# Expert stages of a two-layer block in 12 and 9 units instead of 15 and 10, with products, scatter and gather each in whole runs and six static experts in layer 1

## The chip, the cores and the metric

One core of a Trainium2 chip runs the whole program. The metric is the device time of one execution in microseconds, as the median of three runs. Names of engines: PE is the matrix engine, DVE the vector engine, ACT the scalar engine, POOL the general engine; SP only issues transfers here.

## The reference

Two layers over 256 context rows and 256 latent rows of width 1024. Each layer is a mixer (an RWKV scan in layer 0, differential attention in layer 1) followed by a mixture of experts, and the change is in the experts alone:

```
pg = softmax(h @ router_g + router_g_b)             # 4 groups, the best one is kept
el = (h @ router_e + router_e_b) of that group      # 8 experts, the best two are kept
for g, e:                                           # 32 experts of 1024 -> 256 -> 1024
    hid = silu(h @ w_gate[g, e]) * (h @ w_up[g, e])
    y  += (hid * gates[:, g, e]) @ w_down[g, e]
```

Layer 0 puts 512 rows through this, layer 1 only the 256 latent rows. So 1024 and 512 pairs of row and expert are spread unevenly over 32 experts. An expert's weights are 3 MB in float32, those of a layer 96 MB, and all of them are read in every execution.

## The kernel before

**Units.** An expert gets a fixed number of places (slots) in a unit of 128 places. A unit of kind S holds one expert with 128 slots, P two with 64, Q four with 32. `ORDER` (line 275) gives the kinds in the order of work: 15 units in layer 0, 10 in layer 1. Experts are taken by their rank: the first `STATIC` ones (2 in layer 0, 4 in layer 1) are the experts 0, 1, ... themselves, known when the program is built; the others follow by falling count of rows, and which expert that is only the router tells. What does not fit its slots goes through a loop (`beyond`, from line 2164) with one pass per 64 rows, serial, after the stage.

**Work of a unit.** `onehots` (DVE) compares ranks with slot numbers. `gather` (PE, tile `gp`, line 1862) copies the unit's rows out of the hidden state by products with these one-hot matrices, two units at a time, high and low part of each value apart (`HI`, `LO`), and ACT copies the result into `XG`. `up` (PE, tile `pg`, line 1885) makes the gate and up products in eight steps k of 128 rows each; experts of one unit lie in different column groups of the array, so the four products of a Q step run side by side. `act` (ACT silu, DVE product) gives `hs`, `turn` (PE, tile `ht`) transposes it, `down` (PE, tile `po`, line 1913) makes the last product in two halves, and ACT and DVE scale it into a high and a low part `OB`. `places` (DVE) builds the one-hot matrix `OT` and the gates from `SB` and `WB`, which the rest of the router delivers (`so`, then four PE transposes into `bp`, line 2031). `scatter` (PE, tile `yp`, line 1948, two matmuls per k) brings the unit's output back to the rows, and DVE adds it to `H` (line 1956), for the last units to the block's output `X` (`join`, line 1941).

**Order of the work.** The order is written out by hand in the loop at the end of `moe` and each engine keeps it. In step k of unit s the PE does `up` of s, then `scatter` step k of unit s-2, then one gather step of a coming unit; `turn` and `down` of unit s-1 are put in at k = 1 to 4. The last two units are scattered together.

**Weights.** A load is a third of an expert, 1 MB: c = 0 and 1 are the gate and up weights of four steps each, c = 2 the down weights. All loads go through SP's queue in one order (`expert_loads`) into a ring of buffers, and a load waits until the last reader of the buffer before it is done. In layer 0 the ring has 8 buffers (line 1633). For layer 1 line 1592 adds buffers of the attention stage, 14 in all:

```
more = [(wp, "ah", 2), (wp, "whi", 4)]
ring.pools = more[:1] * 2 + [more[1], ring.pools[0]] * 4 + ring.pools[4:]
```

Loads of static experts are issued before the stage, up to the ring's size; those of the others first read the expert's number (`ids`, DVE cast at line 1801) into a register of SP.

Of the kernel before, what the change touches and what calls it, by code (L numbers as in the profile page):

```python
# [130 lines left out]
STATIC = (2, 4)  # L131
# [143 lines left out]
ORDER = ("PPQSSQSPQSPPPPP", "PPPQQQQQQP")  # L275
# [4 lines left out]
def expert_units(layer):  # L280

    if layer == 1:
        one = []
        two = [(2 * i, 2, 64, 128 * i) for i in range(4)]
        four = [(8 + 4 * i, 4, 32, 512 + 128 * i) for i in range(6)]
    else:
        one = [(2 + i, 1, 128, 128 + 128 * i) for i in range(4)]
        two = [(0, 2, 64, 0)] + [(6 + 2 * i, 2, 64, 640 + 128 * i) for i in range(7)]  # L290
        four = [(20 + 4 * i, 4, 32, 1536 + 128 * i) for i in range(3)]
    kinds = dict(S=one, P=two, Q=four)
    return [kinds[c].pop(0) for c in ORDER[layer]]


def expert_loads(layer):

    us = expert_units(layer)
    out = [(us[0][0], j, 0) for j in range(us[0][1])]
    for n, u in enumerate(us):  # L300
        last = us[n + 1:][:1]
        for v, c in [(u, 1)] * (n + 1 < len(us)) + [(v, c) for v in last for c in range(2 if n + 2 == len(us) else 1)]:
            out += [(v[0], j, c) for j in range(v[1])]
        out += [(u[0], j, 2) for j in range(u[1])]
    return out
# [21 lines left out]
class Prog:  # L327
# [1289 lines left out]
    def open_ring(self):  # L1617
# [21 lines left out]
        def experts(layer, n=32):  # L1639
            return [(load, (layer, r0 + j, c), A["wexp"][layer, r0 + j, :, c * 2048:(c + 1) * 2048])  # L1640
                    for r0, j, c in expert_loads(layer) if r0 < n]
# [13 lines left out]
    def moe(self, layer, TT):  # L1655
# [10 lines left out]
        with ExitStack() as es:  # L1666
# [19 lines left out]
            def rows(i, hf):  # L1686
                tag = ("gu", "gu", "xg", "ht", "po", "po", "y", "gu")[hf * NT + i]
                if tag != "po":
                    tp = pp.tile([P, 512], F32, name="htp", tag=tag, bufs=2 if tag in ("gu", "y") else 1)
# [24 lines left out]
            rp = pp.tile([P, 5, 32], F32, name="rp", tag="y", bufs=2)  # L1714
# [61 lines left out]
            def by_count():  # L1776
# [14 lines left out]
                rt = pp.tile([32, TT], F32, name="rt", tag="y", bufs=2)  # L1791
# [5 lines left out]
                pr = pp.tile([P, NT, 32], F32, name="pr", tag="y", bufs=2)  # L1797
                ip = pp.tile([1, 32], F32, name="ip", tag="y", bufs=2)
# [3 lines left out]
                for i in range(NT):  # L1802
# [4 lines left out]
                ring.todo[i:i + 1] = [(load_dyn, r0 + j, c) for r0, j, c in expert_loads(layer)  # L1807
                                      if r0 >= STATIC[layer]]
# [4 lines left out]
                base = st("base", 32)  # L1813
                if layer == 0:
                    s2, s6, s20 = (st(f"s{n}", 32) for n in (2, 6, 20))
                    for t, n, f in ((s2, 2.0, -64.0), (s6, 6.0, 64.0), (s20, 20.0, 32.0)):
                        nc.vector.tensor_scalar(t, pos, n, f, op0=OP.is_ge, op1=OP.mult)
                    nc.vector.scalar_tensor_tensor(shift, s2, 64.0, s6, op0=OP.add, op1=OP.add)
                    nc.vector.tensor_tensor(shift, shift, s20, OP.add)
                    nc.vector.tensor_scalar(base, shift, -1.0, 128.0, op0=OP.mult, op1=OP.add)  # L1820
                    nc.vector.tensor_tensor(base, base, pos, OP.mult)
                    nc.vector.scalar_tensor_tensor(base, s2, -64.0, base, op0=OP.add, op1=OP.add)
                    nc.vector.scalar_tensor_tensor(base, s6, 5.0, base, op0=OP.mult, op1=OP.add)
                    nc.vector.scalar_tensor_tensor(base, s20, 19.0, base, op0=OP.mult, op1=OP.add)
                else:
                    s8 = own
                    nc.vector.tensor_scalar(s8, pos, 8.0, 32.0, op0=OP.is_ge, op1=OP.mult)
                    nc.vector.tensor_scalar(shift, s8, 64.0, None, op0=OP.add)
                    nc.vector.tensor_scalar(base, shift, -1.0, 128.0, op0=OP.mult, op1=OP.add)
                    nc.vector.tensor_tensor(base, base, pos, OP.mult)  # L1830
                    nc.vector.tensor_scalar(base, base, 64.0, None, op0=OP.subtract)
                    nc.vector.scalar_tensor_tensor(base, s8, 7.0, base, op0=OP.mult, op1=OP.add)
# [6 lines left out]
            def onehots(n):  # L1839
# [4 lines left out]
                r0, nj, w, _ = shapes[n]  # L1844
                of = rkp if r0 >= STATIC[layer] else rk
                o = OHs[g][:, :, h * P:(h + 1) * P].rearrange("p n (e c) -> p n e c", c=w)
                for i in range(NT):
                    nc.vector.tensor_tensor(o[:, i], self.cst("iota")[:, None, 0:w].to_broadcast([P, nj, w]),
                                            of[:, i, r0:r0 + nj, None].to_broadcast([P, nj, w]), OP.is_equal)
# [352 lines left out]
```

## Time and profile before

| | |
|---|---|
| median of 3 runs | 1619.13 us (1616.69 to 1620.01) |
| the profiled execution, its span | 1621.09 us, 1619.3 us |
| PE busy | 1462.1 us (90%) |
| DVE, ACT, POOL busy | 888.7, 602.0, 225.3 us |
| granted PE clock, mean | 0.963 |
| moved by DMA | 355.80 MB, 220 GB/s on average |
| experts of layer 0 | from 779.6 us (first `pg`) to 1109.7 us (last `X`) |
| experts of layer 1 | from 1370.3 us to 1613.4 us, output stored after that |

The span is that of the instructions on the core; the execution's own time is 1.8 us more. Everything between the two expert stages (attention) and before the first is the same in both kernels.

### The profile page before, as it was taken

What the parts mean: (1) busy time and instruction counts of PE and PEld (TensorE: products, weight loads), DVE (VectorE), ACT (ScalarE), POOL (GpSimd) and SP (SyncE); (2) the same over time, 40 slices, a digit from 0 to 9 for tenths busy, and PEclk for the clock granted to TensorE, in tenths of its full rate; (3) what the DMA queues carried; (4) which work ended last, traced back from release to release, by engine and by line L of the source; (5) the groups of instructions that cost most, each with busy time, mean ns of one, the idle gap of its engine ahead of it and who ended that gap; (6) DMA issues with size and microseconds to landing.
All of it is one profiled execution on the core that took longest, in us unless ns stands there. A gap on an engine that the chain in (4) does not pass through costs nothing. (4 is left out here: it accounts for less than half of the span.)

```text
span 1619.3 us, 28356 instructions
## 1 busy us (share of the span) xinstructions
PE 1462.1 (90%) x10935; PEld 785.8 (49%) x10935; DVE 888.7 (55%) x2200; ACT 602.0 (37%) x1260; POOL 225.3 (14%) x345
## 2 busy tenths in 40 slices
PE   5778989999999999988999999986999998998787
PEld 1224445455554565444645445422888885432223
DVE  1746773778778877324735545575555544342224
ACT  3333516355564654324211111105677763211011
POOL 0631212132332331202000000000200001000000
PEclk8999998999999989999999999998999997999999
DMA  8256785766646622343488878782020253799996
GB/s 359 112 199 214 223 268 162 230 203 193 207 158 216 197 85 86 99 135 157 157 329 320 363 293 359 289 330 88 27 102 25 84 183 141 299 373 420 421 421 262
DMA packets 102602, 355.80 MB, mean 220 GB/s; under 512 B 12096, under 2 KB 36032, under 8 KB 74560
## 3 DMA queue, kind: packets, MB, share of 16 engines
q1 hardware_dynamic: 100944, 352.37, 58.9%
q8 instruction: 88, 1.44, 0.4%
q10 hardware_dynamic: 1520, 1.58, 0.3%
q14 instruction: 50, 0.41, 0.1%
HBM read 342.90 MB, written 11.01 MB: 219 GB/s over the span
## 5 line engine op out<-in xcount | busy, mean ns | idle before, releaser
L1885 PE MATMUL pg<-ring,XG 128*32 128x512 f32 (+2 forms) x1024 | 236.1, 615 | 18.5 <-DMA ring<-in_wexp 17.0
L639 PE MATMUL prj<-mxs,wj 128*128 128x512 f32 x288 | 163.4, 650 | 7.0 <-DMA mxs<-mixed 6.9
L1956 DVE TENSOR_TENSOR H<-H,yp 128x512 f32<-128x512 f32 (+1 forms) x152 | 88.7, 588 | 133.8 <-PE yp L1948 133.4
L1948 PE MATMUL yp<-OT,OB 128*128 128x512 f32 (+1 forms) x400 | 129.4, 414 | 2.6 <-DVE X L1941 1.4
L1913 PE MATMUL po<-ring,HT 128*32 128x512 f32 (+2 forms) x512 | 110.2, 622 | 16.2 <-DMA ring<-in_wexp 11.5
L1948 PEld LDWEIGHTS yp<-OT,OB 128*128 128x128 f32 x400 | 61.9, 188 | 118.9 <-issue 45.4
L1917 DVE SCALAR_TENSOR_TENSOR OB<-po,gate,OB 128x512 fp32r<-128x512 f32 x50 | 37.5, 751 | 118.8 <-ACT OB L1916 118.8
L1916 ACT ACTIVATE OB<-po,gate 128x512 fp32r<-128x512 f32 x50 | 34.4, 688 | 180.0 <-PE po L1913 180.0
L1862 PE MATMUL gp<-OH,HI 128*128 128x256 f32 (+1 forms) x352 | 97.5, 308 | 0.0
L996 ACT COPY UV<-pc 64x64 f32<-64x64 f32 x256 | 53.0, 207 | 109.2 <-PE pc L585 86.7
L1862 PE MATMUL gp<-OH,LO 128*128 128x256 f32 (+1 forms) x352 | 89.5, 286 | 0.0
L1862 PEld LDWEIGHTS gp<-OH,HI 128*128 128x128 f32 x352 | 68.7, 195 | 41.3 <-issue 36.2
L1014 POOL TENSOR_SCALAR es<-S,E 128x64 f32<-128x64 f32 x96 | 52.1, 552 | 247.8 <-DVE S L1009 189.8
L367 PE MATMUL gv_ps<-wmod,cst_c 128*32 128x256 f32 (+1 forms) x704 | 62.6, 431 | 25.5 <-DMA wmod<-in_wmod 24.9
L1885 PEld LDWEIGHTS pg<-ring,XG 128*32 128x32 f32 (+2 forms) x1024 | 45.7, 124 | 77.1 <-DMA ring<-in_wexp 36.0
L1866 ACT COPY XG<-gp 128x512 f32<-128x512 f32 (+1 forms) x56 | 30.3, 540 | 124.8 <-PE gp L1862 124.8
L1862 PEld LDWEIGHTS gp<-OH,LO 128*128 128x128 f32 x352 | 69.0, 196 | 2.9 <-issue 1.9
L932 DVE TENSOR_TENSOR xt<-L,X 128x126 f32<-128x126 f32 (+22 forms) x248 | 66.8, 270 | 6.2
L934 DVE TENSOR_TENSOR X<-X,xt 128x126 f32<-128x126 f32 (+22 forms) x248 | 65.1, 263 | 9.0
L639 PEld LDWEIGHTS prj<-mxs,wj 128*128 128x128 f32 x288 | 44.9, 192 | 42.7 <-issue 28.7
L1913 PEld LDWEIGHTS po<-ring,HT 128*32 128x32 f32 (+2 forms) x512 | 28.2, 126 | 71.6 <-issue 39.4
L1275 POOL TENSOR_SCALAR h<-h,sc,mod 128x256 f32<-128x256 f32 x8 | 10.3, 1305 | 365.7 <-DMA ring<-in_wqkv 365.7
(416 smaller groups left out, 2945.9 us busy)
## 6 DMA issues: line engine op xcount, KB each, us to landing
ring<-in_wexp SPq DMA_DIRECT2D x192, 1024.0 KB, 9.2
wmod<-in_wmod SPq DMA_DIRECT2D x80, 512.0 KB, 4.7
mxs<-mixed SPq DMA_DIRECT2D x144, 256.0 KB, 3.7
ring<-in_wqkv SPq DMA_DIRECT2D x12, 1024.0 KB, 5.0
wj<-in_wrkv SPq DMA_DIRECT2D x144, 64.0 KB, 3.2
wmod<-in_wmod SPq DMA_DIRECT2D x8, 1024.0 KB, 10.7
mixed<-mx SPq DMA_DIRECT2D x12, 512.0 KB, 2.7
mf<-mixed SPq DMA_DIRECT2D x12, 512.0 KB, 11.0
```

The costliest lines, as they stand in the source:

```text
L367: nc.tensor.matmul(ps[32 * g:32 * g + 32, u * n:(u + 1) * n], self.cst_c[:, k, :], w[:, g, :], start=(i == 0), stop=(k == 7), skip_group_c ...
L639: nc.tensor.matmul(pj, w, m, start=(k == 0), stop=(k == 7))
L932: nc.vector.tensor_tensor(tv, L[:, s + 1:32, s:s + 1].to_broadcast([P, m, w]), X[:, s:s + 1, 0:w].to_broadcast([P, m, w]), OP.mult)
L934: nc.vector.tensor_tensor(X[:, s + 1:32, 0:w], X[:, s + 1:32, 0:w], tv, OP.add)
L996: nc.scalar.copy(UV[0:64, z, c, h, :], pc[HS[h], 1, :])
L1014: nc.gpsimd.tensor_scalar(es, sn, E[:, z, cf:cf + 1], None, op0=OP.mult)
L1862: nc.tensor.matmul(gp[:, k % 2, c], h[:, i, k // 2, k % 2 * P:k % 2 * P + P], OHs[g][:, i, c], start=(n == 0), stop=(n == 2 * NT - 1))
L1885: nc.tensor.matmul(u.pg[u.w_ * j:u.w_ * (j + 1), :], u.xg(k, j), u.w(j, k // 4)[:, k % 4 * 512:k % 4 * 512 + 512], start=(k == 0), stop=(k ...
L1913: nc.tensor.matmul(u.po[n][js, :], u.HT[:, f, js], u.w(j, 2)[:, f * 1024 + n * 512:f * 1024 + n * 512 + 512], start=(f == 0), stop=(f == 1))
L1917: nc.vector.scalar_tensor_tensor(u.OB[PW, 1, n, :], u.po[n][PW, :], u.gate[PW], u.OB[PW, 0, n, :].bitcast(F32), op0=OP.mult, op1=OP.subtract)
L1948: nc.tensor.matmul(yp, u.OB[PW, h].rearrange("p n d -> p (n d)")[:, k * P:(k + 1) * P], u.OT[PW], start=(i == 0), stop=(i == 2 * len(us) - 1))
L1956: nc.vector.tensor_tensor(h2(k), h2(k), yp, OP.add)
```

## The change

Layer 0 gets 12 units for 15: two new units A hold one frequent expert with 96 slots and one of the two rarest with 32, and there are six units P and four Q. Layer 1 gets 9 units: experts 0 and 1 with 64 slots, the static experts 2 to 5 with 32 each, then six Q units of experts by count, and last the two most frequent ones with 64. `STATIC` becomes (2, 6). In an A unit the first expert's weights are used in three of the four column groups.

The loop does whole runs: all eight steps of `up`, then `act`, then the eight scatter steps of the unit just before (not two before), with four gather steps of a later pair of units among them, `turn` in the middle, then `down`. For the first unit all eight gather steps come before `up` and the next eight after it, among the transposes `bp`. Loads are ordered c = 0, 1, 2 unit by unit. The PSUM buffers move with it: `pg` has one for two, `yp` three for two. The ramps that turn a rank into a slot number have more terms (`steps`), since slots no longer fall with the rank.

```diff
-STATIC = (2, 4)
+STATIC = (2, 6)
...
-ORDER = ("PPQSSQSPQSPPPPP", "PPPQQQQQQP")
+ORDER = ("PAPQPQPQAPQP", "PQQQQQQQP")
...
+        big = []
+        two = [([(0, 64), (1, 64)], 0), ([(6, 64), (7, 64)], 256)]
+        four = [([(2 + i, 32) for i in range(4)], 128)] + [([(8 + 4 * j + i, 32) for i in range(4)], 384 + 128 * j)
+                                                          for j in range(6)]
...
+        big = [([(2 + i, 96), (30 + i, 32)], 128 + 128 * i) for i in range(2)]
+        two = [([(0, 64), (1, 64)], 0)] + [([(4 + 2 * i, 64), (5 + 2 * i, 64)], 384 + 128 * i) for i in range(5)]
+        four = [([(14 + 4 * j + i, 32) for i in range(4)], 1024 + 128 * j) for j in range(4)]
...
+    return [(r, c) for es, _ in expert_units(layer) for c in range(3) for r, _ in es]
...
-                    u.pg = pp.tile([P, 512], F32, name="pg", tag="gu", bufs=2)
+                    u.pg = pp.tile([P, 512], F32, name="pg", tag="gu", bufs=1)
...
-                yp = pp.tile([P, TT], F32, name="yp", tag="y", bufs=2)
+                yp = pp.tile([P, TT], F32, name="yp", tag="y", bufs=3)
...
                 for k in range(KT):
                     up(cur, k)
...
+                    if k % 4 == 3:
+                        more(cur.ne)
+                    if s == 0 and k == 0:
+                        next(bn, None)
+                        onehots(1)
+                        onehots(2)
+                    elif s == 0 and k in (2, 3, 5):
+                        next(rr)
+                    elif s and k == 1:
+                        places(cur)
...
+                act(cur)
+                if s == 0:
+                    side = [lambda k=k: gather(1, k) for k in range(KT)]
+                    for k, f in enumerate(side):
+                        f()
+                        if k in (1, 2, 3, 4):
+                            next(rr)
+                        if k == 4:
+                            places(cur)
+                        if k == 2:
+                            turn(cur)
+                else:
+                    g, h = divmod(s + 3, 2)
+                    side = [lambda k=k: gather(g, k) for k in range(h * 4, h * 4 + 4)] if 2 * g - 1 < N else []
+                    for k in range(KT):
+                        scatter(k, last)
+                        if k in (0, 1, 4, 5) and side:
+                            side.pop(0)()
+                        if k == 3:
+                            turn(cur)
+                for n in range(2):
+                    down(cur, n)
+                more(cur.ne)
+                last = cur
             for k in range(KT):
-                scatter(k, mid, cur)
+                scatter(k, last)
```

The order of instructions on the PE, at the end of layer 0's stage. Before, the last rows of the last unit (`pg` and `yp` alternate eight times, of which one pair stands here), with both last units' `down` and scatter behind it:

```order
L1885 MATMUL pg<-ring,XG 64x512 x2
L1948 MATMUL yp<-OT,OB 128x512 x2
L1898 MATMUL ht<-consts,hs 128x128 x2
L1913 MATMUL po<-ring,HT 64x512 x16
L1948 MATMUL yp<-OT,OB 128x512 x32
```

The same place now, from the `down` of the last but one unit (a Q) to the end of the stage:

```order
L1920 MATMUL po<-ring,HT 32x512 x16
L1894 MATMUL pg<-ring,XG 64x512 x16
L1955 MATMUL yp<-OT,OB 128x512 x8
L1907 MATMUL ht<-consts,hs 128x128 x2
L1955 MATMUL yp<-OT,OB 128x512 x8
L1920 MATMUL po<-ring,HT 64x512 x8
L1955 MATMUL yp<-OT,OB 128x512 x16
```

So the products of a unit stand together, and so do the scatter matmuls of the unit before it.

The PE at the start of layer 0's stage. Before, the first product of the first unit follows four gather steps, and further gather steps (`gp`) stand between the products:

```order
L1862 MATMUL gp<-OH,LO 128x128
L1885 MATMUL pg<-ring,XG 64x512 x2
L1799 MATMUL ip<-bcs,consts 1x32
L1803 MATMUL pr<-bcs,rts 128x32 x4
L1862 MATMUL gp<-OH,HI 128x128
```

Now the matmul for the expert numbers (`ip`) comes behind all eight gather steps, and the products follow it in one piece, with only the router's `ep` in between:

```order
L1868 MATMUL gp<-OH,LO 128x128
L1793 MATMUL ip<-bcs,consts 1x32
L1797 MATMUL pr<-bcs,rts 128x32 x4
L1894 MATMUL pg<-ring,XG 64x512 x12
L2005 MATMUL ep<-consts,EUc 1x128
L1894 MATMUL pg<-ring,XG 64x512 x4
L1868 MATMUL gp<-OH,HI 128x256
```

SP's queue ahead of layer 1's stage, before (attention's weights, then the loads of static experts, then the first number of an expert):

```order
L1637 DMA ring<-in_wqkv 128x2048 x8
L1637 DMA ring<-in_wo 128x2048 x4
L1637 DMA ring<-in_wexp 128x2048 x12
L2076 TENSOR_LOAD ids
L2076 ISA x2
```

The same place now:

```order
L1631 DMA ring<-in_wqkv 128x2048 x8
L1631 DMA ring<-in_wo 128x2048 x4
L1631 DMA ring<-in_wexp 128x2048 x18
L2083 TENSOR_LOAD ids
L2083 ISA x2
L2158 TENSOR_LOAD nun
```

Six more loads stand ahead of the first that needs a number, and the count of passes of the overflow loop (`nun`) is now read right behind it.

## Rows read from the trace of the kernel before

**Rows 1.** Stretches (us): busy time of each engine, granted PE clock, DMA share, GB/s.
```profile
780.00:1110.00 330.00, 316.01 (x1546) 151.12 (x1542) 178.59 (x412) 53.06 (x99) 0.00 (x0) 0.99 0.76 299
900.00:930.00 30.00, 30.00 (x158) 15.42 (x158) 15.94 (x35) 4.65 (x9) 0.00 (x0) 1.00 1.01 422
1345.00:1373.00 28.00, 22.33 (x118) 17.84 (x119) 15.23 (x51) 10.23 (x19) 5.43 (x6) 0.75 0.14 54
1373.00:1400.00 27.00, 25.59 (x118) 12.84 (x118) 11.69 (x57) 6.98 (x17) 0.00 (x0) 0.82 0.65 240
1400.00:1440.00 40.00, 39.28 (x210) 15.84 (x210) 15.21 (x41) 8.13 (x15) 0.00 (x0) 1.00 0.88 346
1440.00:1600.00 160.00, 133.98 (x748) 43.61 (x748) 49.42 (x138) 17.39 (x35) 0.00 (x0) 0.98 1.01 421
```

**Rows 2.** The chain that ended last: start, length, what.
```profile
1518.58 19.80 DMA ring<-in_wexp
```

**Rows 3.** PE timeline, layer 0: a step of an S, then of a P unit.
```profile
865.23 1.02 PE L1885 MATMUL pg<-ring,XG 128*128 128x512 f32 x2
...
866.55 1.02 PE L1885 MATMUL pg<-ring,XG 128*128 128x512 f32 x2
...
1066.34 1.08 PE L1885 MATMUL pg<-ring,XG 128*64 128x512 f32 x4
...
1068.01 1.08 PE L1885 MATMUL pg<-ring,XG 128*64 128x512 f32 x4
```

**Rows 4.** PE timeline, layer 0: five steps of `up`, six of `down` in a run.
```profile
786.62 4.51 PE L1885 MATMUL pg<-ring,XG 128*64 128x512 f32 x20
791.06 0.38 PE L1998 MATMUL ep<-consts,EUc 128*1 128x128 f32 x2
...
1094.33 5.37 PE L1913 MATMUL po<-ring,HT 128*64 128x512 f32 x24 [1.58 <-DVE OB L1917]
1099.63 2.11 PE L1948 MATMUL yp<-OT,OB 128*128 128x512 f32 x8
```

**Rows 5.** PE timeline, layer 0: first of eight gather matmuls, and what follows.
```profile
861.65 0.28 PE L1862 MATMUL gp<-OH,HI 128*128 128x256 f32 x1
...
862.59 1.02 PE L1885 MATMUL pg<-ring,XG 128*128 128x512 f32 x2
```

**Rows 6.** DMA issues: count, KB each, median us to landing.
```profile
ring<-in_wexp SPq DMA_DIRECT2D x192, 1024.0 KB, 9.2
```

**Rows 7.** DVE timeline, start of layer 0: expert numbers, slot numbers of the rows.
```profile
780.85 0.18 DVE L1801 CAST ids<-ip 1x32 int32<-1x32 f32 x1 [0.98 <-PE ip L1799]
...
798.47 0.29 DVE L2018 TENSOR_REDUCE so<-ov 128x4 f32<-128x128 f32 x1
```

**Rows 8.** PE timeline, start of layer 0: first gather, wait for the slot numbers.
```profile
775.89 0.31 PE L1862 MATMUL gp<-OH,HI 128*128 128x128 f32 x1
...
798.82 0.65 PE L2031 MATMUL bp<-consts,so 128*128 128x128 f32 x4 [0.43 <-DVE so L2018]
```

**Rows 9.** PE timeline, end of layer 0: two steps of `down` after a wait.
```profile
1088.77 0.44 PE L1898 MATMUL ht<-consts,hs 128*128 128x128 f32 x2 [2.91 <-DVE sid L1923]
1089.13 3.62 PE L1913 MATMUL po<-ring,HT 128*64 128x512 f32 x8
```

**Rows 10.** DVE timeline: last additions to `X` in layer 0 and in layer 1.
```profile
1107.84 1.81 DVE L1941 SCALAR_TENSOR_TENSOR X<-yp,mod,X 128x256 f32<-128x256 f32 x4 [0.43 <-PE yp L1948]
...
1612.46 0.96 DVE L1941 SCALAR_TENSOR_TENSOR X<-yp,mod,X 128x256 f32<-128x256 f32 x2 [0.36 <-PE yp L1948]
```

**Rows 11.** Groups by line, 850 to 1060 us, DVE: busy us, mean ns, idle before.
```profile
L1956 DVE TENSOR_TENSOR H<-H,yp 128x512 f32<-128x512 f32 x82 | 55.7, 686 | 65.0 <-PE yp L1948 64.6
```

**Rows 12.** PE timeline, start of layer 1: first gather, first product, later products.
```profile
1366.68 0.45 PE L1862 MATMUL gp<-OH,HI 128*128 128x128 f32 x1
...
1370.26 1.98 PE L1885 MATMUL pg<-ring,XG 128*64 128x512 f32 x4
...
1379.05 6.30 PE L1885 MATMUL pg<-ring,XG 128*64 128x512 f32 x20
```

More of the change, by code (lines that the diff above doesn't have):

```diff
@@ L1806, in by_count @@
                 i = ring.todo.index("further")
-                ring.todo[i:i + 1] = [(load_dyn, r0 + j, c) for r0, j, c in expert_loads(layer)
-                                      if r0 >= STATIC[layer]]
+                ring.todo[i:i + 1] = [(load_dyn, r, c) for r, c in expert_loads(layer) if r >= STATIC[layer]]
                 more(2)
@@ new lines, in steps @@
+                def steps(to, *terms):
+                    for (s_, f), prev in zip(terms, [None] + [to] * len(terms)):
+                        if prev is None:
+                            nc.vector.tensor_scalar(to, s_, f[0], f[1], op0=OP.mult, op1=OP.add)
+                        else:
+                            nc.vector.scalar_tensor_tensor(to, s_, f, prev, op0=OP.mult, op1=OP.add)
+                at_ = (2, 4, 14, 30) if layer == 0 else (2, 6, 8)
+                sst = xp.tile([P, 4, 32], F32, name="sst", tag="OT", bufs=2)
@@ new lines, in by_count @@
+                ss_ = [sst[:, i, :] for i in range(len(at_))]
+                for t, n in zip(ss_, at_):
+                    nc.vector.tensor_scalar(t, pos, float(n), 32.0, op0=OP.is_ge, op1=OP.mult)
+                slope = own
+                if layer == 0:
+                    s2, s4, s14, s30 = ss_
+                    steps(shift, (s2, (-1.0, 64.0)), (s4, 1.0), (s14, 1.0))
+                    steps(slope, (s2, (2.0, 64.0)), (s4, -2.0), (s14, -1.0), (s30, 3.0))
+                    steps(base, (s2, (-3.0, -64.0)), (s4, 7.0), (s14, 13.0), (s30, -131.0))
+                else:
+                    s2, s6, s8 = ss_
+                    steps(shift, (s2, (1.0, 64.0)), (s6, -1.0), (s8, 1.0))
+                    steps(slope, (s2, (-1.0, 64.0)), (s6, 1.0), (s8, -1.0))
+                    steps(base, (s2, (1.0, -64.0)), (s6, -5.0), (s8, 7.0))
@@ L1873, in unit @@
                 u.n, u.po = n, {}
-                r0, u.nj, u.w_, u.base = shapes[n]
+                es_, u.base = shapes[n]
+                u.ne, u.w_ = len(es_), min(w for _, w in es_)
+                of = [r for r, w in es_ for _ in range(w // u.w_)]
+                u.nj = len(of)
                 u.PW = slice(0, P)
-                u.w = lambda j, c: ring.got[layer, r0 + j, c]
+                u.w = lambda j, c: ring.got[layer, of[j], c]
                 XG, h = XGs[(n + 1) // 2], (n + 1) % 2 * P
@@ L2090, in moe @@
             rr = rest_of_router()
-            units = []
+            last = None
             for s in range(N):
-                units.append(unit(s))
-                cur, mid, old = (units[i] if i >= 0 else None for i in (s, s - 1, s - 2))
-                g, h = divmod(s + 3, 2)
-                side = []
+                cur = unit(s) if s else None
                 if s == 0:
                     next(bn, None)
-                    for k in range(4):
+                    for k in range(KT):
@@ L2134, in moe @@
-                    k0 = 3 + (s == 1)
-                    if mid is not None and k in (k0 - 1, k0) and s < N - 1:
-                        down(mid, k - k0 + 1)
-                    if k in (k0, 7):
-                        more(cur.nj + (mid.nj if mid is not None and k == k0 and s < N - 1 else 0))
-                    for f in side.pop(0) if side else ():
-                        f()
-                    if s == 1 and k < 2:
-                        next(rr)
-                        next(rr)
@@ L2144, in moe @@
-                act(cur)
-            turn(cur)
-            places(cur)
-            for n in range(2):
-                down(mid, n)
-            more(mid.nj)
-            for n in range(2):
-                down(cur, n)
-            more(cur.nj)
+                    if k % 4 == 3:
+                        more(cur.ne)
+                    if s == 0 and k == 0:
+                        next(bn, None)
+                        onehots(1)
[4 more added lines that the diff above has]
+                        places(cur)
+                    elif s % 2 and k == 4:
+                        for n in (s + 2, s + 3):
+                            if n < N:
+                                onehots(n)
```

110 lines of the change are left out of this document (28 added, 82 removed).

## The prediction

> **What bounds the kernel now.** First the stretches [rows 1]. In layer 0's expert stage (780 to 1110 us) the PE is busy 316 of 330 us at a clock of 0.99, while DMA reaches 0.76 of its share; in a part of it (900 to 930) loads do run at 422 GB/s, so more is to be had. 330 us for 15 units are 22.0 us each: this stage is the PE's. In layer 1 the stretch 1440 to 1600 has a DMA share of 1.01 and 421 GB/s with PE gaps, and the chain of waits consists there of loads, 19.8 us at a time [rows 2]: DMA's stage. Its beginning isn't: 54 GB/s from 1345 to 1373, then 240 and 346. A load has 1024 KB [rows 6], so at 421 GB/s it takes 1.0486 MB / 421 = 2.49 us, and the 96 loads of a layer 239 us.
>
> Then a unit's price on the PE. A step of `up` and a scatter pair, alternating, take 1068.01 - 1066.34 = 1.67 us in a P unit but 1.32 us in an S unit, which uses the array whole [rows 3]. Five P steps in a run take 791.06 - 786.62 = 4.44 us, 0.89 each, and `down` has 0.88 [rows 4]. So a scatter pair is 1.32 - 0.89 = 0.43, and changing between split and whole array in each step costs 1.67 - 1.32 = 0.35, eight times per unit. A gather matmul is (862.59 - 861.65) / 8 = 0.118 [rows 5].
>
> **The change, part by part.**
>
> *A unit in runs*: 8 x 0.89 for `up`, 8 x 0.43 for scatter, 32 x 0.118 for half a pair's gather, 0.3 for the transpose [rows 9], 4 x 0.88 for `down`: 7.1 + 3.4 + 3.8 + 0.3 + 3.5 = 18.1; with two changes of the array (0.7) 18.8 us. An A unit isn't in the trace; below it is the run's 0.89, above it the 1.32 of an S step less its scatter, which is the same 0.89: I take that.
>
> *The first unit of layer 0* gets slower. Gather starts as before at 775.9; eight steps of eight matmuls at 0.11 (half as wide) end at 783.0. `ip` and `pr` take 1.3 us, `up` runs from 784.3 to 791.5, two gather steps of the next pair end at 793.4. Then `bp` needs `so`, and `so` hangs on a DVE chain that begins with the cast of the numbers: it lasts from 780.85 to 798.76, 17.9 us [rows 7], and before, the PE came to `bp` just in time (idle 0.43 [rows 8]). Now the cast is at 783.4, and seven small operations more for the ramps (0.2 each) and four more pieces of one-hot (A has two widths) stand in the chain, against some 2 us of waiting for ACT in it that shrink: 802. The PE is idle for 8.6 us. Behind the stall are four `bp`, six gather steps, the transpose and short waits for copies, 9.2 us, and 2.3 us for a low clock: after an idle time of 2.9 us two steps of `down` took 3.62 us where 1.77 is normal [rows 9]. With `down` the unit ends at 817 (bounds 812 and 822).
>
> *The next two units*, A and P, need 12 loads, 30 us, and 37.6 us of PE: the PE's. They end at 855.
>
> *The rest* is DMA's: the ring of 8 is full at 855 and three units have used 18 loads, so 96 - 26 = 70 are to come, 174 us: 1029. A Q and a P together need 44.8 us of loads and 37.6 of PE, so DMA doesn't stop there, but behind the second A comes a P, 29.9 against 37.6, and the ring can't take more: a stop of 8 to 10. The last load lands at 1038.
>
> *The end of layer 0.* The last unit's c = 1 loads land 5 us earlier, and its `up` ends 1037. Scatter of the unit before adds to `X`, 0.9 us per k on DVE (1.81 for two k [rows 10]), with three buffers `yp`: the PE is through at 1043, `down` at 1047. The second half of `OB` takes 1.5 us more, eight last steps at 0.9 end at 1056. Before, the last addition ended at 1109.65 [rows 10]: **53.6 us gained**. The attention weights' loads follow the experts' directly and land ahead of their reader.
>
> *Layer 1.* Its gain is at its beginning. The ring has 14 buffers, but only 12 static loads: two now come early, four more need no number. The first gather runs at half clock, (1370.26 - 1366.68) / 16 = 0.22 per matmul [rows 12], ends 1373.8, `up` follows at 1374.9 with steps of 1.9 until the clock returns (five steps in 6.3 us then [rows 12]) and ends at 1386; so the first buffers come free at 1382.5, as before. Eight gather steps, `bp` and copies: 1393, `down` 1396.5. Here `so` is there in time: the layer has half the rows. Until then DMA fetches four loads; from then on four buffers at a time come free, and the other 78 loads run through: 1396.5 + 2 + 194 = 1593. The tail: `down` behind the scatter of the unit before ends 1599, `OB` and eight additions of 0.48 end 1604, and as the PE comes to it from long waits I add 3 for a low clock: 1607, against 1613.4 [rows 10]. **6.4 us gained.**
>
> A page speaks against part of this: the Trainium skill, "DMA: Bandwidth & Descriptors", Specifications, gives a limit of about 358 GB/s for a core's HBM. By that a load would take 2.93 us and the 148 loads of both DMA stretches 65 us more, and the gain would be gone; the 421 and 422 GB/s of [rows 1] differ, and the measurement decides.
>
> *Costed at nothing*: `places`, one-hots and `H` additions, 11 us of DVE in 18.8 us of PE; one `pg` buffer, since ACT and DVE have read it while scatter runs (8 us); the read of `nun` on SP ahead of the first numbered load of layer 1, which waits for its buffer until 1396 anyhow, while `nun` is cast near 1388. If DVE's cover were gone, an `H` addition (0.69 [rows 11]) for 0.43 of scatter would cost 8 x 0.26 = 2 us per unit.
>
> **Sum**: 53.6 + 6.4 = 60.0. The profiled execution took 1621.1 us, 2.0 above the median; so 1561 for a profiled one, **1559 us** as a median.
>
> **The rivals.**
>
> *DMA runs through in layer 0* (no stall at `bp`, no stop at A and P). For it: the ring runs eight loads ahead. Against: the DVE chain of [rows 7]. From 782.5, 90 loads take 224 us, plus the tail of 18: 1025, a gain of 85, with layer 1 some 92: 1527 at best, 1538 in the middle.
>
> *Runs lay chains open.* Within a run nothing covers a wait: gather steps share one PSUM buffer and wait for ACT's copy, scatter waits for DVE, `down` for `HT`. For it: [rows 11], the one buffer `xg`. Against: gather and scatter steps alternate. 2.5 us per unit, 30 in all: 1589.
>
> *The clock falls (slower).* Runs of products with waits for loads between them could keep the PE at 1.2 GHz; [rows 9] and the first products of [rows 12] show it after waits, and what it costs. At 1.2 GHz throughout, layer 0's units take 37 us: 783 + 12 x 37 = 1227, 118 later than now, 1730 in all. It decides from about 54 us of PE work at the low clock in units that have no slack, a quarter of the stage's 225. Against: 0.98 in the DMA-bound 1440 to 1600 [rows 1], with gaps there too. The page "TensorE: Matmul & The Clock Gate", section "HAM oscillation — how this bites in real kernels", of the Trainium skill describes this very thing, bursts that each start at the low clock because of a DMA wait; the 0.98 does not agree so far.
>
> *The capacity isn't enough.* An expert with more rows than slots starts the serial loop: three loads, gather, products and scatter one after the other, about 31 us per pass from the same rows, so two passes eat the gain. The reference's own routing on its inputs gives no pass: in layer 0 77 and 69 rows for 96 slots, at most 59 for 64, 31 for 32; in layer 1 at most 24 (static) and 30 for 32, 39 for 64.
>
> **Chances.** Forecast (gain 45 to 75) 0.57, DMA through 0.15, open chains 0.20, clock 0.04, capacity 0.01, no effect 0.03. Within 0.2% (3 us, about what a measurement here can tell from no change) 0.03, slower 0.05, faster 0.92. The range takes in the middle of the first rival and the second: 1532 to 1590.
>
> **What would show it.** Right: 18 to 20 us per unit in layer 0's first half, then 410 GB/s or more; `pg` steps of 0.89 in runs; an idle PE of about 8 us ahead of the first `bp`; last `X` of layer 0 at 1056, and in layer 1 a DMA share of 1 from about 40 us earlier in the stage. Wrong: PE busy with gaps behind `XG`, `yp` or `HT` in each unit, a clock under 0.9 in the expert stages, DMA under 380 GB/s from 860 on, or instructions on the tile `gpu`.

## The result, and the profile after it

The changed kernel took 1572.91 us (median of 4 runs, 1565.39 to 1577.41), the kernel before 1617.91 beside it (4 runs): a ratio of 0.9719, interval 0.9674 to 0.9763, 45 us gained of the 60 that were forecast. The profiled execution is the fastest of the four, 1565.4 us with a span of 1563.6; against the profiled one of before it is 55.7 us shorter.

First the stretches of the kernel after, in the columns of [rows 1]: the first unit of layer 0, the next two, the units up to 970, a pair of A and P, the end; then the beginning of layer 1, its middle and its tail.

```profile
772.00:812.00 40.00, 32.52 (x219) 22.00 (x222) 24.47 (x92) 9.70 (x20) 0.00 (x0) 0.96 0.41 158
812.00:852.00 40.00, 36.78 (x244) 19.57 (x236) 21.53 (x46) 6.19 (x12) 0.00 (x0) 1.00 0.79 315
852.00:970.00 118.00, 102.62 (x632) 51.60 (x634) 54.87 (x123) 16.52 (x30) 0.00 (x0) 0.99 0.99 408
970.00:1011.00 41.00, 37.73 (x252) 19.70 (x244) 20.70 (x42) 6.18 (x12) 0.00 (x0) 1.00 0.90 364
1011.00:1064.00 53.00, 42.02 (x230) 18.17 (x228) 34.65 (x79) 5.69 (x11) 0.00 (x0) 1.00 0.78 317
1319.00:1350.00 31.00, 27.27 (x174) 14.94 (x177) 18.05 (x83) 9.05 (x20) 0.00 (x0) 0.97 0.45 170
1350.00:1400.00 50.00, 38.21 (x266) 15.04 (x262) 14.82 (x44) 6.61 (x12) 0.00 (x0) 0.96 1.01 420
1400.00:1540.00 140.00, 103.23 (x612) 37.45 (x606) 38.58 (x107) 15.35 (x28) 0.00 (x0) 0.92 1.01 421
```

Layer 0 now has, from its fourth unit on, DMA nearly full and gaps on the PE, and so has layer 1 from 1350 on. But look at 812 to 852: no lack of loads yet (DMA 0.79), and still the PE is idle for 3.2 of 40 us. What it waits for stands in the groups of the page (line, names, count; busy us, mean ns; idle time ahead, and what ended it):

```profile
L1920 PE MATMUL po<-ring,HT 128*32 128x512 f32 (+1 forms) x544 | 85.2, 612 | 38.4 <-DVE OB L1924 35.9
```

and in the PE's timeline of layer 0's second unit, an A (start, length, what; in brackets the idle time and its releaser):

```profile
811.44 7.07 PE L1894 MATMUL pg<-ring,XG 128*32 128x512 f32 x64
...
826.41 1.92 PE L1920 MATMUL po<-ring,HT 128*32 128x512 f32 x16
829.93 1.92 PE L1920 MATMUL po<-ring,HT 128*32 128x512 f32 x16 [1.59 <-DVE OB L1924]
831.78 0.65 PE L1894 MATMUL pg<-ring,XG 128*64 128x512 f32 x2
```

`up` takes 7.07 us as forecast. `down` doesn't: its second half starts only when ACT and then DVE have made `OB` out of the first half, 1.59 us later, in every unit: in layer 0 the PE is idle 21.4 us for `OB` in 12 places, and 9.2 us for loads ahead of `pg`. The bracket of [rows 4] is the same wait; before, it stood at two places of layer 0 in all, since `up` and gather steps lay between the halves.

The first gather of layer 0, the waits of the first unit, and the last additions to `X` in either layer (PE and DVE timelines; these answer to [rows 7, 8, 10]):

```profile
772.29 0.31 PE L1868 MATMUL gp<-OH,HI 128*128 128x128 f32 x1
...
789.06 0.59 PE L2005 MATMUL ep<-consts,EUc 128*1 128x128 f32 x2 [2.98 <-DVE EUc L2002]
...
796.79 0.65 PE L2038 MATMUL bp<-consts,so 128*128 128x128 f32 x4 [2.01 <-DVE so L2025]
```

```profile
779.81 0.18 DVE L1795 CAST ids<-ip 1x32 int32<-1x32 f32 x1 [3.61 <-PE ip L1793]
...
796.45 0.29 DVE L2025 TENSOR_REDUCE so<-ov 128x4 f32<-128x128 f32 x1
...
1057.38 6.35 DVE L1948 SCALAR_TENSOR_TENSOR X<-yp,mod,X 128x256 f32<-128x256 f32 x16
...
1553.89 3.22 DVE L1948 SCALAR_TENSOR_TENSOR X<-yp,mod,X 128x256 f32<-128x256 f32 x8
```

From the first gather to the last addition layer 0 takes 1063.73 - 772.29 = 291.4 us (before 333.8), and layer 1, whose first gather is at 1319.39, 237.7 (before 246.7): 42.3 and 9.0 us gained. The forecast said 53.6 and 6.4. (Of the 9.0, up to 7 may be the clock's and not the change's, as the experiments show below.) The other 4.4 us between the two profiles lie outside the changed stages: the first gather of layer 0 comes 3.6 us earlier, behind code that the change doesn't touch.

At the end of layer 1 the wait stands in the chain itself (start, length, what). `down` of the last unit but one waits for ACT and DVE in the middle (its first half, 3.36 us for what takes 1.92 behind it, also ran at the lower clock for the most part):

```profile
1529.73 3.36 PE po L1920 x16
...
1533.16 0.70 ACT OB L1923
...
1533.88 0.76 DVE OB L1924
...
1534.69 1.92 PE po L1920 x16
1536.61 7.04 PE pg L1894 x32
```

### The profile page after: what moved, and what is told of

It reads as the page before. It is cut to its first block, busy times and chain, and to the rows that moved or that the text cites. A ratio compares the mean times of both kernels' runs of the same rounds, so it can differ in the third digit from the quotient of the medians.

```text
span 1563.6 us, 28143 instructions
## 1 busy us (share of the span) xinstructions
PE 1355.9 (87%) x10863; PEld 751.6 (48%) x10863; DVE 858.2 (55%) x2157; ACT 588.9 (38%) x1236; POOL 224.3 (14%) x345
## 3 DMA queue, kind: packets, MB, share of 16 engines
q10 hardware_dynamic: 1520, 1.58, 0.3%
## 5 line engine op out<-in xcount | busy, mean ns | idle before, releaser
L1894 PE MATMUL pg<-ring,XG 128*32 128x512 f32 (+1 forms) x1088 | 195.8, 643 | 42.4 <-DMA ring<-in_wexp 42.4
L1894 PEld LDWEIGHTS pg<-ring,XG 128*32 128x32 f32 (+1 forms) x1088 | 51.0, 123 | 181.6 <-issue 104.8
L1920 PE MATMUL po<-ring,HT 128*32 128x512 f32 (+1 forms) x544 | 85.2, 612 | 38.4 <-DVE OB L1924 35.9
L1955 PE MATMUL yp<-OT,OB 128*128 128x512 f32 (+1 forms) x336 | 87.5, 365 | 5.1 <-DVE X L1948 2.6
L361 PE MATMUL gv_ps<-wmod,cst_c 128*32 128x256 f32 (+1 forms) x704 | 62.5, 431 | 24.1 <-DMA wmod<-in_wmod 23.8
L1963 DVE TENSOR_TENSOR H<-H,yp 128x512 f32<-128x512 f32 (+1 forms) x120 | 66.1, 577 | 26.5 <-PE yp L1955 26.5
L1868 PE MATMUL gp<-OH,HI 128*128 128x256 f32 (+1 forms) x304 | 76.4, 285 | 2.1 <-ACT XG L1872 2.0
L1868 PE MATMUL gp<-OH,LO 128*128 128x256 f32 (+1 forms) x304 | 75.3, 281 | 0.0
L1955 PEld LDWEIGHTS yp<-OT,OB 128*128 128x128 f32 x336 | 51.4, 189 | 31.2 <-issue 18.8
L1920 PEld LDWEIGHTS po<-ring,HT 128*32 128x32 f32 (+1 forms) x544 | 19.5, 117 | 90.6 <-DVE OB L1924 55.3
L1868 PEld LDWEIGHTS gp<-OH,HI 128*128 128x128 f32 x304 | 58.0, 191 | 6.7 <-ACT XG L1872 3.2
L1868 PEld LDWEIGHTS gp<-OH,LO 128*128 128x128 f32 x304 | 58.0, 191 | 1.9
```

The source lines that it names most:

```text
L361: nc.tensor.matmul(ps[32 * g:32 * g + 32, u * n:(u + 1) * n], self.cst_c[:, k, :], w[:, g, :], start=(i == 0), stop=(k == 7), skip_group_c ...
L1868: nc.tensor.matmul(gp[:, k % 2, c], h[:, i, k // 2, k % 2 * P:k % 2 * P + P], OHs[g][:, i, c], start=(n == 0), stop=(n == 2 * NT - 1))
L1894: nc.tensor.matmul(u.pg[u.w_ * j:u.w_ * (j + 1), :], u.xg(k, j), u.w(j, k // 4)[:, k % 4 * 512:k % 4 * 512 + 512], start=(k == 0), stop=(k ...
L1920: nc.tensor.matmul(u.po[n][js, :], u.HT[:, f, js], u.w(j, 2)[:, f * 1024 + n * 512:f * 1024 + n * 512 + 512], start=(f == 0), stop=(f == 1))
L1955: nc.tensor.matmul(yp, u.OB[PW, h].rearrange("p n d -> p (n d)")[:, k * P:(k + 1) * P], u.OT[PW], start=(i == 0), stop=(i == 2 * len(us) - 1))
L1963: nc.vector.tensor_tensor(h2(k), h2(k), yp, OP.add)
```

## The experiments

**The theory** after this reading: what fell short is one term, `down`, because `po` is one PSUM tile of two banks. The second half writes another bank than ACT and DVE read, but the wait is on the tile. **The rivals**: loads set the pace from the fourth unit on, so that the wait is hidden; the runs never paid, and the gain is the fewer units'; the first unit's stalls are what failed.

All medians below are beside the kernel before on the same chip (1618.11 us in 17 runs in the first set, 1621.78 in 11 in the second; the second set is the runs and the units with two tiles, the other order and the late static loads, and medians of different sets are compared by their ratios). The stages are read as above, from the first gather matmul to the end of the last addition to `X`:

| kernel | median us | ratio to before | layer 0 | layer 1 |
|---|---|---|---|---|
| before | 1618.1 | | 333.8 | 246.7 |
| runs alone | 1618.3 | 0.9998 (0.9967 to 1.003) | 341.8 | 240.8 |
| units alone | 1576.8 | 0.9722 (0.9652 to 0.9793) | 307.0 | 232.4 |
| both: the change, again | 1575.2 | 0.9740 (0.9691 to 0.9789) | 291.8 | 237.9 |
| runs, two tiles | 1584.9 | 0.9778 (0.9728 to 0.9827) | 312.4 | 233.7 |
| units, two tiles | 1567.4 | 0.9666 (0.9617 to 0.9715) | 304.6 | 232.0 |
| **both, two tiles** | **1546.2** | **0.9563 (0.9509 to 0.9618)** | **275.4** | **233.3** |
| both, two tiles, other order | 1547.3 | 0.9549 (0.9508 to 0.9591) | 273.9 | 232.6 |
| the change, late static loads | 1565.2 | 0.9671 (0.9622 to 0.9719) | 294.5 | 237.8 |

The 246.7 us of layer 1 before have to be read with care. That kernel was profiled once, and in that execution layer 1 began at a low clock. Its first 20 us from the first gather, then those of the units alone, which have the same interleaved loop:

```profile
1367.00:1377.00 10.00, 10.00 (x39) 6.52 (x37) 3.87 (x19) 1.33 (x4) 0.00 (x0) 0.50 0.25 77
1377.00:1387.00 10.00, 10.00 (x39) 4.27 (x38) 6.20 (x29) 0.57 (x3) 0.00 (x0) 0.72 0.64 243
```

```profile
1340.00:1350.00 10.00, 10.00 (x68) 6.35 (x68) 8.10 (x38) 1.91 (x7) 0.00 (x0) 1.00 0.01 2
1350.00:1360.00 10.00, 8.59 (x56) 3.88 (x53) 6.00 (x28) 3.53 (x7) 0.00 (x0) 1.00 0.96 360
```

The first `down` starts 31.2 us behind the first gather there (1397.83 - 1366.68) and 23.8 us behind it with the units alone (1364.37 - 1340.62). So up to 7 us of what any kernel of the table gains in layer 1 on the 246.7 may be this clock; how long layer 1 of the kernel before takes without it was not measured.

**`po` as two tiles.** In `down`, and alike where `rows` borrows the tag:

```
-                if n == 0:
-                    po = pp.tile([P, 2, 512], F32, name="po", tag="po", bufs=1)
-                    u.po = [po[:, i, :] for i in range(2)]
+                if n == 0:
+                    u.po = {}
+                u.po[n] = pp.tile([P, 512], F32, name="po", tag=f"po{n}", bufs=1)
```

> The two halves of `down` get a PSUM tile of one bank each; the bytes and banks are the same. Theory 1, that the wait of the second half for the first half's `OB` (1.6 us in each unit) is part of the price of a unit: it goes in all 12 units, a unit in runs costs 18.8 us instead of 20.4, and the units in which PE sets the pace (some six of layer 0, the first two of layer 1, both ends) get shorter: layer 0 by 8 to 11 us, layer 1 by 2 to 4, about 1560. Rival, that DMA hides it: loads set the pace behind the third unit, and what PE gains there it waits for loads: only the three first units and the last one of layer 0 and the tail of layer 1 show it, 3 to 6 us in all, about 1568.

It took 1546.23 us, 29 less than the changed kernel beside it; between the profiles it is 23.7 (spans of 1562.7 and 1539.0). That is more than even the theory said: 16.4 us in layer 0, 4.6 in layer 1. Its group of the page, the PE's timeline of the same unit, and stretches of layer 0 (first unit, next two, the units up to 956, the pair of A and P):

```profile
L1915 PE MATMUL po<-ring,HT 128*32 128x512 f32 (+1 forms) x544 | 82.9, 607 | 3.6 <-DMA ring<-in_wexp 3.6
```

```profile
820.81 3.64 PE L1915 MATMUL po<-ring,HT 128*32 128x512 f32 x32
824.38 1.08 PE L1889 MATMUL pg<-ring,XG 128*64 128x512 f32 x4
```

```profile
768.00:806.00 38.00, 32.38 (x217) 22.16 (x219) 24.67 (x92) 9.30 (x20) 0.00 (x0) 0.96 0.43 166
806.00:843.00 37.00, 37.00 (x248) 19.93 (x244) 21.54 (x46) 6.59 (x12) 0.00 (x0) 1.00 0.85 341
843.00:956.00 113.00, 104.29 (x636) 51.47 (x637) 54.63 (x123) 16.52 (x30) 0.00 (x0) 0.98 1.00 415
956.00:994.00 38.00, 37.58 (x248) 19.95 (x241) 20.60 (x43) 6.18 (x12) 0.00 (x0) 1.00 1.01 418
```

No wait for `OB` is left. `down` takes 3.57 us instead of 831.78 - 826.41 = 5.37, and from 806 to 843 the PE is never idle: two units in 37 us, 18.5 each. The saving also shows where the theory had loads hide it (113 and 38 us for 118 and 41): the ring has only eight buffers, a load starts when `down` or `up` has read one, so a PE that is 1.8 us late makes the loads late (408 and 364 GB/s against 415 and 418). The Trainium skill, "PSUM — Partial Sum Buffer", section "PSUM bank collisions raise a hardware error", says to guard PSUM by bank and quadrant of partitions, not by address; the halves lie in different banks, so by that rule too the wait wasn't needed, and the trace of the two tiles (`po` in one piece of 3.64 us) agrees.

**Each half of the change alone.** Units alone: the loop, the order of loads and the PSUM buffers of before, with the change's units, ramps and `STATIC`. Runs alone: the change's loop, order and buffers with the units, ramps and `STATIC` of before. As a diff of the tables that differ:

```
 units alone, against before             runs alone, against the change
-STATIC = (2, 4)                         -STATIC = (2, 6)
+STATIC = (2, 6)                         +STATIC = (2, 4)
-ORDER = ("PPQSSQSPQSPPPPP", ...)        -ORDER = ("PAPQPQPQAPQP", ...)
+ORDER = ("PAPQPQPQAPQP", ...)           +ORDER = ("PPQSSQSPQSPPPPP", ...)
```

> The kernel before, its interleaved loop and its order of loads, with the new units (12 and 9, six static experts, the new ramps). Theory 1, that fewer units are the gain and the runs are not: a unit costs the 22.0 us of before, 12 of them 264, and with the ends of before layer 0's experts take about 268 us (334 less 3 x 22), 23 less than the changed kernel; DMA allows 250; so about 1550. Theory 2, that the runs carry a good part: a pair of Q and P needs 44 us of PE in interleaved steps and 45 us of loads, neither has slack, each wait of one for the other is lost, a unit costs 24 to 25, layer 0 takes 295 to 300 us: 1575 to 1582.

> The changed kernel's loop and order of loads with the old units (15 and 10, four static experts, the old ramps). Theory 1, with a unit in runs at 20.4 us because of the wait in `down`: 39 us for the first unit, 14 x 20.4, 8 for the last scatter, less some 4 because the four S units change no array: 328 to 333 us against 334 before, and layer 1 as before: 1610 to 1618. The prediction's price of 18.8 a unit would give 39 + 14 x 18.8 + 8 - 3 = 307 us and some 1592.

The units alone took 1576.84 us, as theory 2 had it: the pairs of Q and P have no slack in interleaved steps (the PE waits 14.8 us for loads in layer 0). The runs alone took 1618.27, a ratio of 0.9998: nearer to theory 1. But both sums came out by misses that cancel: layer 0 took 307.0 and 341.8 us where 295 to 300 and 328 to 333 were expected, and layer 1 took 14 and 6 us less than before, which neither expectation had and of which up to 7 is the clock above. So the time of the change is, to within its error, that of its units alone, and yet the change isn't its units: in layer 0 runs save 307.0 - 291.8 = 15 us on top of them, and in layer 1 they cost 237.9 - 232.4 = 5.5. ("Runs" is the loop, the order of loads and the PSUM buffers together; no run takes these three apart.)

**Two tiles with each half alone.** The same edit of `down` in these two kernels.

> The runs with the old units, and `po` as two tiles. Theory 1: the old units in runs gained nothing because the wait of `down` (24.3 us of idle time ahead of `po` in layer 0's stretch) ate what the runs gave; without it layer 0's PE-bound units give it all back, 22 to 24 us there and 1 to 3 in layer 1: 1590 to 1596. Rival, that the runs were at their limit for another reason (first unit, loads in whole thirds): 1608 or more.

> The new units in the interleaved loop, and `po` as two tiles. Theory 1, that the wait belongs to the runs: interleaved, the PE has `up` and gather steps between the halves, the idle time ahead of `po` for `OB` is only 2.2 us in layer 0 and 1.6 at each end; so 0 to 4 us less than the 1577 of the new units alone: 1573 to 1577. Rival, that separate tiles pay in either order, some 20 us as in the runs: 1555.

1584.86 and 1567.35 us. The wait belongs to the runs: two tiles take 29.4 us off layer 0 with the runs alone, 16.4 off the change, and 2.4 with the units alone. What ended the PE's idle time ahead of `po` in layer 0 (us, times), of the runs alone and of before (the line of `OB` is each kernel's own):

```profile
  DVE OB L1916: 24.3, 15
```

```profile
  DVE OB L1917: 2.3, 2
```

With two tiles the runs are worth 333.8 - 312.4 = 21 us with the old units and 304.6 - 275.4 = 29 with the new, where with one tile they cost 8 and gave 15 (the kernel before has one tile, but waits only the 2.3 us of the row above for it). The runs with two tiles came out 5 us below their expectation: 29.4 us of layer 0 against 24.3 of idle time, and 7.1 of layer 1 where 1 to 3 were expected. Part of the 29.4 is that each half starts anew: two halves apart take 1.92 + 1.92 us, both in a piece 3.64, 0.2 per unit or 3 in 15. Another 1.0 lies in the first unit, 40.3 us against 37.6 with 1.8 for the wait and the new start, at a clock of 0.86 against 0.95; for the rest I have no row. The units with two tiles came out 6 us below their expectation, but their two stages only 2.8 us shorter, as expected; what else is gained lies outside them (the first gather comes 5.1 us earlier).

**Layer 1's static loads.** The change knows experts 4 and 5 of layer 1 without the router. Here they are fetched by number instead, all else as in the change:

```
-... for c in range(4)] + experts(1, STATIC[1]) + ["further"]
+... for c in range(4)] + experts(1, 4) + ["further"]
...
-        ring.todo[i:i + 1] = [(load_dyn, r, c) for r, c in expert_loads(layer) if r >= STATIC[layer]]
+        ring.todo[i:i + 1] = [(load_dyn, r, c) for r, c in expert_loads(layer) if r >= (2, 4)[layer]]
```

> The changed kernel, with the six loads of layer 1's static experts 4 and 5 fetched by number, behind the router, as those of the further experts; units, slots and order stay. The prediction put layer 1's gain down to these loads, two early, four without a number: then about 5 us are lost, 1578 to 1580. Theory 2, that they come no earlier because they are issued in the program behind the router in either kernel and wait for buffers, and that the gain is that of nine units for ten: 0 to 1.5 us, 1573 to 1576.

Layer 1 took 237.8 us in the profile, the change's 237.7: theory 2. (The median of 1565 is lower than the change's 1575 of another set; layer 1 doesn't explain it, and the span of its profile, 1562.0, is the change's.) Stretches of 10 us from the first gather of layer 1, of this kernel:

```profile
1318.00:1328.00 10.00, 10.00 (x62) 6.31 (x61) 6.12 (x36) 2.00 (x7) 0.00 (x0) 0.93 0.35 118
1328.00:1338.00 10.00, 7.85 (x50) 5.15 (x49) 6.99 (x33) 5.09 (x10) 0.00 (x0) 1.00 1.02 426
1338.00:1348.00 10.00, 8.43 (x62) 2.77 (x64) 4.00 (x13) 1.96 (x3) 0.00 (x0) 1.00 0.50 183
1348.00:1358.00 10.00, 9.19 (x82) 5.21 (x70) 3.98 (x13) 2.61 (x5) 0.00 (x0) 1.00 1.01 420
```

and of the change, the third of these stretches:

```profile
1339.00:1349.00 10.00, 8.23 (x56) 3.05 (x60) 3.94 (x13) 2.10 (x4) 0.00 (x0) 1.00 0.30 96
```

In both kernels DMA runs out of free buffers some 20 us behind the first gather and is full 30 us behind it. Loads that come earlier only make this hole bigger (0.30 against 0.50).

**Another order.** Two tiles, and in layer 0 a Q as the second unit in place of an A, so that DMA has more to fetch early:

```
-ORDER = ("PAPQPQPQAPQP", "PQQQQQQQP")
+ORDER = ("PQPPQPAQPAQP", "PQQQQQQQP")
```

> Two tiles for `po`, and layer 0's units in the order P Q P P Q P A Q P A Q P. Theory: the first three units (P, A, P) need only 18 loads in 75 us, DMA is at 166 and 341 GB/s there and full from the fourth unit on; with a Q second, DMA is full some 35 us earlier and moves some 7 us' worth of loads more by then: 1539, and the rest of the stage waits less for loads. Rival: a Q needs 12 loads and the ring holds 8, so that the early Q waits for its last loads and PE loses what DMA gains: 1546 as with the old order, or a little more.

1547.29 us: nothing gained, the rival. DMA is indeed full earlier (first row below: second and third unit, 405 GB/s where it had 341), but then runs at 402 where it had 415, and the PE's wait for loads ahead of `pg` is 11.3 us in either kernel.

```profile
810.00:847.00 37.00, 33.65 (x210) 16.82 (x203) 18.31 (x42) 5.22 (x10) 0.00 (x0) 1.00 0.99 405
847.00:960.00 113.00, 107.12 (x676) 54.96 (x677) 58.41 (x133) 18.47 (x33) 0.00 (x0) 0.98 0.98 402
```

**Half loads.** Is the rest of a unit's time the loads'? In the change, and in the version with two tiles:

```
-                fetch(regs[r], c, ring.got, (layer, r, c))
+                ring.got[layer, r, c] = third()
+                nc.sync.dma_start(ring.got[layer, r, c][:, 0:1024], ...[:, c * 2048:c * 2048 + 1024])
...
-    u.w(j, k // 4)[:, k % 4 * 512:k % 4 * 512 + 512]
+    u.w(j, k // 4)[:, k % 2 * 512:k % 2 * 512 + 512]
```

> The changed kernel with numbered loads of half the size (512 KB; the products read the half that is there twice, so that the output is another). Theory 1, that loads set the pace from layer 0's fourth unit on and in all of layer 1: without them layer 0 takes 39 us for its first unit, 11 x 20.4 and 8 for the last scatter, 271 instead of 291; in layer 1 a unit needs 7.1 + 4.3 + 5.5 = 16.9 us of PE, the layer 26 + 8 x 16.9 + 5 = 166 instead of 238: some 92 us less in all, about 1475. Rival, that layer 0 is held by its own waits (DVE, ACT, array) and not by loads: 291 stays there, and only layer 1 gets shorter: about 1495.

> The same half loads with `po` as two tiles. Theory: a unit of layer 0 costs 18.5 us in every place, the layer 37 + 11 x 18.5 + 7 = 248 instead of 275; layer 1's units 7.1 + 4.3 + 3.7 = 15.1, the layer 25 + 8 x 15.1 + 5 = 151 instead of 233: about 1430. The difference to the half loads with one tile is then the wait alone, 23 us in layer 0 and 15 in layer 1. Rival, that another wait stands behind the first (OB on DVE before scatter, the transposes): a unit stays above 20 and the difference is under 15 in layer 0.

1511.42 and 1473.52 us, one run each, where 1475 and 1430 were expected; most of what is missing is a pass of the serial loop that was not reckoned with. Layer 0 takes 280.3 and 253.9 us (expected 271 and 248). Layer 0's other output gives layer 1 another routing, under which that pass runs; up to that pass layer 1 takes 162.9 and 151.6 (expected 166 and 151). So in layer 1 the loads are 75 us of the change's 238, and in layer 0 only 11 of 291: there the PE's units and the wait are nearly all (the PE waits for loads for 0.8 us in all of it). One tile against two is 26.4 us in layer 0 and 11 in layer 1: the wait, no longer hidden by anything. The pass itself begins with the gather on `gpu`, in the PE's timeline of the second kernel:

```profile
1432.43 0.42 PE L2067 MATMUL gpu<-uh,HI 128*128 128x64 f32 x1 [2.30 <-DVE uh L2061]
```

The last addition ahead of the loop ends at 1430.74, the last in it at 1465.35: 34.6 us for a pass, where the rival of the capacity had worked out 31.

**The change three times more.**

> The changed kernel again, as the measure for its neighbours: about 1573 us, layer 0's experts (first gather to last addition to X) 291 us, layer 1's 238 us, as in its first profile (1565 us). Its four times so far spread over 12 us, those of before over 5. If loads set the end of both expert stages now, a part of this should be the rate they get: at 417 for 421 GB/s the 150 loads in them take 3.6 us more, and a slower profile should show it in the stretches where DMA is full. If instead waits in the first units or the clock vary, the difference stands before 860 us or at the layer's end, with the same rate.

> The changed kernel once more, one profile. Its six timed runs lie between 1564 and 1580 us, the slower the lower the mean granted clock (0.964 to 0.948). If the clock is what differs, a profile at a lower clock shows longer spells at 1.2 GHz, and the time is lost where they fall on units that PE holds up; the rate of loads stays 420 GB/s. If it is memory, the rate is lower. A profile at 0.964 again says nothing.

> The same as the one before it, a second chance of a profile at a lower clock: 1564 to 1580 us.

1575.15 us (six runs, 1564.46 to 1579.68), and 1567.54 and 1575.78 in one run each. The last was profiled at a granted clock of 0.954 and tells where the time of a longer execution is. Its first gather of layer 0, and the same row of the first repetition, at 0.964:

```profile
779.82 0.31 PE L1868 MATMUL gp<-OH,HI 128*128 128x128 f32 x1
```

```profile
770.99 0.31 PE L1868 MATMUL gp<-OH,HI 128*128 128x128 f32 x1
```

8.8 of the 11.3 us are gone before the experts begin, 2.6 more in layer 0 (294.4), none in layer 1 (237.7). In front of that first gather the clock was lower; 600 to 768 us in the longer one, then in the other:

```profile
600.00:768.00 168.00, 151.93 (x1183) 79.67 (x1182) 73.67 (x220) 57.86 (x137) 29.94 (x50) 0.92 0.34 115
```

```profile
600.00:768.00 168.00, 151.43 (x1204) 82.48 (x1202) 79.16 (x242) 59.75 (x140) 31.50 (x52) 0.95 0.34 115
```

## Why the prediction came out as it did

The time lies in the range and the sign is right, at the lower edge of the forecast of 45 to 75 by the medians, but the gain of 60 was too big by 15 in the medians and by 9 (51.3 against 60.0) in the two changed stages. Step by step:

- **The price of a unit.** The term that was mis-sized is `down`, costed at 4 x 0.88 = 3.5 us from [rows 4]: measured 5.4, because of the wait for `OB`. With it a unit costs 831.78 - 811.44 = 20.3 us instead of 18.8, and without it, in the version with two tiles, 18.5. All other terms of the price were right. I divided the row's 5.37 us of work into steps and passed over the bracket behind it, 1.58 us idle; where a wait stands once, at the end of a stage, since other work covers it everywhere else, taking the cover away puts it into each unit. The row misled in one more way: in the kernel before the last unit's two halves have PSUM tiles of their own (line 1904, tag `gu`), so that 16 of its 24 matmuls are a `down` without the wait. The change took these tiles away with the second `pg` buffer, and the last unit then waits as well (1.62 us at 1053.98). The rival of open chains asked for such a wait, but behind `XG`, `yp` and `HT`: these have 3.0 us of idle time in all of layer 0.
- **The first unit** took 811.44 - 772.29 = 39.2 us where 41.1 were forecast. The chain on DVE from the cast to `so` takes 16.9 us, not the 18.6 worked out for it, and part of the wait comes at `ep`, in the middle of `up`, where it wasn't looked for: idle 2.98 + 2.01 instead of 8.6. These 3.6 us less are half eaten by the 1.9 more in `down`.
- **The next two units** are the PE's, an A costs what a P does (20.3 and 20.4), and they end 79.9 us behind the first gather, against 79.1.
- **The rest is DMA's**: half right. DMA is at 408 GB/s, the stop at A and P came (364), but with half-sized loads only 11 us of the layer go. With eight buffers neither engine is the bound alone: what the PE loses, the loads lose in part with it, and a lateness of 1.8 us per unit is only partly hidden: it is worth 26.4 us with half loads and still 16.4 with whole ones.
- **The end of layer 0**: 291.4 us behind the first gather instead of 280.1, so 11.3 are missing. The wait is worth 291.4 - 275.4 = 16.0 there by the version with two tiles, so the other terms were 4.7 too long. That they made up for a part of the wait is luck.
- **Layer 1**: 237.7 us instead of 240.3, and DMA is full 30 us behind the first gather (30 to 32 forecast). That this fits is in part luck. The forecast took the low clock of [rows 12] over, with `up` of the first unit ending 19.3 us behind the first gather; in the change the first 10 us are at 0.90 and `up` ends 13.6 us behind it (1332.96 - 1319.39), and `down` with its wait takes a part of that back. The reason given for the gain was wrong: loads without a number, early or not, are worth nothing here. The nine units alone give all of it and more (232.4), less the up to 7 us that are the clock's; the runs with one tile give 5.5 back.
- **The clock** stayed a rival that didn't come: 0.96 to 1.00 in layer 0. In layer 1 it is 0.92 from 1400 to 1540, but there DMA is full at 421 GB/s, and the end is the loads'. Behind waits for loads of 1.4 us the PE is at either level there: the last 26 matmuls of an `up` take 3.62 us at 1459.30 and 6.58 at 1489.10. The Trainium skill, "TensorE: Matmul & The Clock Gate", section "HAM oscillation — how this bites in real kernels", describes bursts that each start at the low clock because of a wait for DMA; the trace agrees for some bursts of layer 1 and not for most, and with 0.99 hardly in layer 0.
- **The limit of 358 GB/s** that was weighed in the prediction does not hold here: 420 and 421 GB/s in layer 1 again. The Trainium skill, "HBM Reference", section "Specifications (TRN2)", has it as the share of a core when both of a pair stream, and about 425 for one that streams alone; the traces agree with the latter.
- **Medians and profiles**: the gain is 55.7 us between the profiled executions and 45.0 between the medians. The profiled one of the change was its shortest, that of before lay 3.2 us above its median, and the repeated profiles show where a longer one loses its time: mostly ahead of the experts (first gather at 771.0 and at 779.8 in the same kernel). Whether the change makes such executions likelier stays open: it wasn't profiled below a clock of 0.954.

## What to carry to other kernels

A tuned loop hides waits that its trace then shows once or twice; before work is sorted into runs, look at what each step in a run waits for from the step just before it, and take the idle time in a row's bracket into the price. A PSUM tile of two banks is one thing to wait for; two tiles of one bank each cost the same space and let the second half run while the first is read (here 21 us in the two stages, and 29 of 1575 between the medians). And a ring of few buffers ties engine and loads together: in such a stage a microsecond lost on either side is not simply hidden behind the other (16 of 26 us were lost here).

## What the runs showed of the chip

Runs of one program differ by up to 24 us here, and the time follows the mean granted clock: of 17 runs of the kernel before, the one at 0.976 took 1603.66 us and the one at 0.957 took 1626.61; of six of the change, 0.964 went with 1564.46 and 0.948 with 1579.68. The size fits, as an estimate: 0.019 of 1620 us is 62 us at 1.2 GHz instead of 2.4, 31 of them lost if the PE was the bound there, and 23 are. In the one profile of such an execution of the change most of this time was lost ahead of the code under study; in the one profile of the kernel before a part was lost inside it, at the start of layer 1. So two kernels are better compared by their stages, from one named row to another, than by a single execution's time, and with the granted clock of each stage beside them.
